# Scaling softmax weights by their reciprocal sums before their transposes, in a hand-scheduled two-layer diffusion block

## The chip, the core and the metric

The kernel runs on one core of a Trainium2 chip. The metric is device time in microseconds (us), from three timed runs before the change; beside them stands one profiled execution of the same program, from which every duration below is read. PE is TensorE (matmuls and transposes), PEld its weight loads, DVE is VectorE, ACT is ScalarE, POOL is GpSimd and SP is SyncE; the last two issue the DMAs here. All engines execute their own instructions strictly in the order in which the program lists them.

## The reference

Two layers of a block with two parallel branches over 512 latent tokens and 256 context tokens, width 1024. The change touches the attention branch alone: 8 query heads in two key groups, head width 128.

```
s = einsum('bqhgd,bkhd->bhgqk', q_blk, keys) * scale
p = softmax(s, axis=-1)
o = einsum('bhgqk,bkhd->bqhgd', p, vals)
```

Latent queries see all 768 keys, context queries only the 256 context keys. Layer 0 needs both kinds of query, layer 1 only the latent ones. The rest (input projection, rotary turns, a long convolution through Fourier tables, gates, output projection, SwiGLU feed-forward) is the same before and after.

## The kernel before

Activations lie with channels on the partitions and tokens along the free axis. Every large product runs as three matmuls (`mm3`): each operand is split in a high part and a low part, and hi·hi, hi·lo and lo·hi are summed in one PSUM tile. A split (`split`) is one ACT copy (the high part) and one DVE subtraction (the low part).

The order of the work is not written by hand. The kernel is a set of Python generators: one main `program`, one per weight load, attention lanes, rotary chunks, splits. A class `Order` keeps a rough clock for each engine. A generator yields what its next step needs (tiles written, free slots of a tile pool, events); among those that can go on, the one with the lowest priority number does. Splits have -5, attention lanes 4, the main program 5, so lanes go ahead of query projections and gates whenever they are ready, and the main program fills what they leave. The result is one fixed order for each engine. Whatever changes an attention step's cost, needs or slots can therefore change the order of everything beside it.

Slots: 37 tiles `s` of 768 columns, 13 tiles `f` and a few others of 1024, 8 PSUM tiles `ps`. Layer 1 needs four `s` slots for each of its four query chunks; each attention unit takes two for its weights `Ps`.

An attention unit (`attn_part`) is one head and 256 queries, as two blocks of 128 (i = 0, 1). There are 24 units in layer 0 (16 latent, 8 context) and 16 in layer 1, all latent: 32 latent and 8 context units in all. A unit's steps:

1. Scores, queries on the partitions: for a latent unit twelve matmuls into three PSUM tiles (`ps<-f,s`, widths 512 and 256, since keys lie in `f` tiles and queries in `s` tiles).
2. Maxima (`mx`), negated and scaled (`nb`) on DVE; exponentials on ACT into `Ps`, their row sums into `sm`.
3. The reciprocal sums `ri` on DVE (`ri<-sm`, `ri<-ri`).
4. For each pair of key tiles four transposes of the weights (`ps<-ident,s`), a split of the result into an `f` tile, and six matmuls with the values (`ps<-f`, width 256), which sum up the output O, head channels on the partitions and queries along the free axis.
5. After the last of them the reciprocal sums, one number for each query, are spread over the partitions by two more transposes (`ps<-ident,ri`), copied by ACT to `rb` (in the slot of `Ps[0]`), multiplied into O by DVE, and the result is split into the query's own tile: ACT `qh`, DVE `ql`. Then the slots are given back, and the lane takes its next unit.

Beside the lanes run the main program's query chunks (`tok_chunk`, `ps<-hi,s` and `ps<-lo,s`, width 256), the rotary chunk of each (`rope_chunk`: on DVE a sum of squares `ss`, ten small instructions on `rs` and `rq`, four passes over 1024 columns), the gates and merges (`ps<-s,hi`, `ps<-s,lo`), and the splits of the arriving weights (`lo<-raw,hi`).

Of the kernel before, what the change touches and what calls it, by code (L numbers as in the profile page):

```python
# [19 lines left out]
P = 128  # L20
# [44 lines left out]
class Order:  # L65
    """Puts the work of several generators into one program order.

    A generator yields what its next step needs: tiles that were written, free
    slots ("tag", n) or Events. Rough costs of the instructions emitted so far
    say when these are there; of the generators that can go on, the one with  # L70
    the lowest priority number does.
    """

# [5 lines left out]

    @staticmethod  # L80
    def span(ap):
        step = ap.ap[0][0]
        lo = ap.offset % step if step else ap.offset
        return ap.tensor.name, lo, lo + 1 + sum((n - 1) * abs(st) for st, n in ap.ap[1:])

# [15 lines left out]
    def run(self, eng, cost, outs, ins, late=0.15, born=None, after=0.0):  # L101
        start = max(self.now[eng], after)
        if born is not None:
            start = max(start, self.born.get(born.tensor.name, 0.0))
        for ap in ins:
            if ap.tensor.name in self.writes:
                start = max(start, self.after(ap, eng))
        for ap in outs:
            start = max(start, self.born.get(ap.tensor.name, 0.0))
        end = start + cost  # L110
        self.now[eng] = end
        for ap in ins:
            n = ap.tensor.name
            self.used[n] = max(self.used.get(n, 0.0), end)
        for ap in outs:
            n, lo, hi = self.span(ap)
            w = [x for x in self.writes.get(n, ()) if not (lo <= x[0] and x[1] <= hi)]
            self.writes[n] = w + [(lo, hi, end, late, eng)]
            self.used[n] = max(self.used.get(n, 0.0), end)
# [7 lines left out]
    def give(self, tag, i, tile_):  # L127
        self.free[tag].append((self.used.get(tile_.tensor.name, 0.0), i))

# [57 lines left out]
RING = 4096  # L187
SLOTS = {"raw": 5, "hi": 4, "lo": 4, "s": 37, "f": 13, "ps": 8}


def hyena_body(ctx, tc, I, out):
# [6 lines left out]

    # ------------------------------------------------------------- tiles and instructions
    def new(tag, dt=F32, n=None):  # L200
        kept = tag == "s"
        od.kept += kept
        tag = {"t": "s"}.get(tag, tag)
        size = {"s": TOK, "ps": 512}.get(tag, 1024)
        p = psp if tag == "ps" else sp
        free, i = od.take(tag)
        t = p.tile([P, n or size], dt, tag=f"{tag}{i}", name=tag)
        od.born[t.tensor.name] = free
        tags[t.tensor.name] = tag, i, kept
        return t  # L210

    def drop(*tiles):
        for t in tiles:
            tag, i, kept = tags[t.tensor.name]
            od.kept -= kept
            od.give(tag, i, t)
# [71 lines left out]
    def rsqrt(y, u):  # L288
        """y becomes (u / RS) ** -0.5."""
        t = cst.tile(list(u.shape), F32, tag="rq", name="rq", bufs=2)  # L290
        ts(y.bitcast(I32), u.bitcast(I32), 1, ALU.logical_shift_right)
        ts(y.bitcast(I32), y.bitcast(I32), -1.0, ALU.mult, float(0x5F3759DF), ALU.add)
        tt(t, y, y, ALU.mult)
        tt(t, t, u, ALU.mult)
        stt(t, t, -10.0 / 3.0, t, ALU.add, ALU.mult)
        stt(y, t, 5.0, y, ALU.add, ALU.mult)
        stt(t, y, -0.5 / RS, y, ALU.mult, ALU.mult)
        tt(t, t, u, ALU.mult)
        stt(y, t, 1.5, y, ALU.add, ALU.mult)
# [5 lines left out]

    # ------------------------------------------------------------- weights, in the order of use
    plan = []
# [61 lines left out]

    # ------------------------------------------------------------- constants  # L370
    silc = cst.tile([P, KD, 2], F32, name="silc")
# [11 lines left out]

    # ------------------------------------------------------------- modulation
    mod = [[cst.tile([P, 48], F32, name=f"mod{l}{s}") for s in range(2)] for l in range(DEPTH)]
# [78 lines left out]

    # ------------------------------------------------------------- norm
    class Sums:
        """The squares of a residual's tiles, summed as they become final."""

# [68 lines left out]

    # ------------------------------------------------------------- projections
    def spans_of(nt):
# [49 lines left out]
    def parts(acts, seg, kept, stay, end, evac):  # L589
        """The output tiles for a part of the tokens; weights that stay serve the next part, first of all."""  # L590
        if kept:
# [8 lines left out]

    # ------------------------------------------------------------- hyena filters
    h3_dram = tc.dram_tile([FH, SEQ], F32, name="h3d")
# [44 lines left out]
    class Tabs:  # L647
        """DFT tables, two of 2 KB a slot: the odd ones stay, the even ones are swapped."""

# [112 lines left out]

    # ------------------------------------------------------------- hyena branch
    hy_dram = [tc.dram_tile([P, 4, TOK], F32, name=f"hyd{l}") for l in range(DEPTH)]
# [149 lines left out]

    # ------------------------------------------------------------- q, k, v
    def tok_chunk(h, nt, evac):
# [102 lines left out]

    # ------------------------------------------------------------- attention  # L1020
    def attn_part(q, kT, v, kvh, q0, k0):
        qh, ql = q
# [25 lines left out]
        for i in range(2):  # L1048
            act(Ps[i][:, c0:c0 + CTX], Sc[:, 256 * i:256 * i + 256], AF.Exp, scale=SCALE, bias=nb[:, i:i + 1],
                accum_out=sm[:, 0, i:i + 1])  # L1050
        drop(Sc, *Sl)
        if lat:
            tt(ri, sm[:, 0, :], sm[:, 1, :], ALU.add)
            recip(ri, ri)
        else:
            recip(ri, sm[:, 0, :])
        hs = slice(HD * kvh, HD * kvh + HD)
        O = None
# [5 lines left out]
        def pv(kp):  # L1064
            pt = pts[kp]
            for kk in range(2):
                kt = k0 // P + 2 * kp + kk
                c = slice(256 * kk, 256 * kk + 256)
                mm3(O[:, 0:256], v[0][kt][:, hs], v[1][kt][:, hs], pt[0][:, c], pt[1][:, c],
                    kp == 0 and kk == 0, kp == nk // 2 - 1 and kk == 1)  # L1070
            drop(pt[0])

        for kp in range(nk // 2):
# [9 lines left out]
            if kp:  # L1083
                if O is None:
                    yield [("ps", 1)]
                    O = new("ps")
                yield list(pts[kp - 1]) + vs(kp - 1)
                pv(kp - 1)
        if O is None:
            yield [("ps", 1)]  # L1090
            O = new("ps")
        yield list(pts[-1]) + [ri] + vs(nk // 2 - 1)
        pv(nk // 2 - 1)
        for i in range(2):
            tr(O[:, 256 + P * i:256 + P * i + P], ri[:, i:i + 1].to_broadcast([P, P]))
        rb = Ps[0]
        act(rb[:, 0:256], O[:, 256:512])
        yield [rb[:, 0:256]]
        tt(rb[:, 0:256], O[:, 0:256], rb[:, 0:256], ALU.mult)
        drop(O)  # L1100
        yield [rb[:, 0:256]]
        act(qh[:, q0:q0 + 256], rb[:, 0:256])
        yield [qh[:, q0:q0 + 256]]
        tt(ql[:, q0:q0 + 256], rb[:, 0:256], qh[:, q0:q0 + 256], ALU.subtract)
        drop(*Ps)

    def attn_lane(units, qT, kT, v, left, done, after):
        while units:
            hd, part = units.pop(0)
            yield [ev for ev in after[hd]]  # L1110
            yield from attn_part(qT[hd], kT[hd // 4], v, hd // 4, 256 * part, 0 if part < 2 else SEQ)
            left[hd] -= 1
            done[hd].set = left[hd] == 0

    # ------------------------------------------------------------- layers
    gate_dram = [tc.dram_tile([16, P, TOK], F32, name=f"gated{l}") for l in range(DEPTH)]
# [100 lines left out]
    def program():  # L1217
# [29 lines left out]
        for l in range(DEPTH):  # L1247
# [3 lines left out]
            stag = ((0, 256), (256, 512)) if last else ((0, SEQ), (SEQ, TOK))  # L1251
            # norm, hyena columns
            if l == 0:
# [4 lines left out]
            if l == 0:  # L1258
                # the residual's loads go before those of the tables
                yield [xs[-1][:, SEQ:TOK]]  # L1260
# [23 lines left out]
            for j in islice(gates, EARLY[l]):  # L1284
                yield from gate_job(l, h, nt, j)
            # q, k, v
            stop.set = True
# [18 lines left out]
            yield from tok_chunk(h, TOK, v_evac)  # L1306
            # attention beside the queries and gates
            qT = []
# [24 lines left out]
            yield [here]  # L1333
            # merge, output projection
            if l == 0:
# [24 lines left out]
            drop(*[x for p in mg for x in p])  # L1360
            # feed-forward
            for gi, (f0, fn) in enumerate(GROUPS):
# [86 lines left out]

# ---------------------------------------------------------------- host layout  # L1450
def _split(x64):
# [125 lines left out]
```

## Time and profile before

| | |
|---|---|
| Timed runs | 2189.72, 2190.36, 2190.59 us; median 2190.36 us |
| Profiled execution, span from first to last instruction | 2187.6 us |
| PE busy | 2146.5 us, 98% |
| DVE busy | 1365.3 us, 62% |
| ACT busy | 744.3 us, 34% |
| Layer 0, 285 to 625 us: PE, DVE, ACT busy | 337.06, 222.42, 151.81 us |
| Layer 1, 1500 to 1730 us: PE, DVE, ACT busy | 225.75, 149.91, 117.98 us |

The profile gives the profiled execution by its span alone; the median of the timed runs lies 2.8 us above that span. The two windows hold nearly all of the attention. A busy time merges overlapping instructions, and consecutive instructions of one engine do overlap in the trace, so the cost of one in a run of equals is the distance between starts and not its duration.

### The profile page before, as it was taken

The page shows a single profiled execution, that of the slowest core. Times are in us where ns is not written, and L with a number is a line of the kernel's source. Part 1 is how long each engine was busy: PE and PEld are TensorE (multiplying, and loading weights), DVE is VectorE, ACT ScalarE, POOL GpSimd, SP SyncE. Part 2 cuts the span into 40 slices and gives each one's busy share as a digit, 9 for nine tenths or more (in the row PEclk, how much of TensorE's full clock was granted, in tenths as well). Part 3 has the DMA queues.
Part 4 walks back from the last instruction along what each step waited for, and adds up shares of the span by engine and source line. Part 5 has one row for each costly group of instructions (what it writes and reads, how often), then busy time and mean ns, then how long its engine had stood idle before and what let it go on. Part 6 is the DMA issues. An engine that isn't in the chain of part 4 may idle for free.

```text
span 2187.6 us, 31896 instructions
## 1 busy us (share of the span) xinstructions
PE 2146.5 (98%) x12849; PEld 1888.5 (86%) x12849; DVE 1365.3 (62%) x2510; ACT 744.3 (34%) x1350; POOL 116.8 (5%) x218
## 2 busy tenths in 40 slices
PE   7999999999999999999999999999999999999997
PEld 2889999999888888888888887899888898888887
DVE  5879766665796799733333477766756666434345
ACT  3432234444522421121221334224455443222222
POOL 2111100000100000000000011200001000000000
PEclk9999999999999999999999999999999999999999
DMA  9334521112465257812112232522213433323221
GB/s 327 100 117 151 192 81 46 37 51 80 152 229 183 78 196 239 306 44 74 65 50 82 102 111 91 182 85 73 102 49 121 158 111 99 106 83 111 80 95 57
DMA packets 83060, 256.84 MB, mean 117 GB/s; under 512 B 10668, under 2 KB 15183, under 8 KB 82912
## 3 DMA queue, kind: packets, MB, share of 16 engines
q1 hardware_dynamic: 63840, 197.43, 26.7%
q0 software_dynamic: 19072, 57.36, 8.0%
q8 instruction: 101, 1.65, 0.3%
q14 instruction: 47, 0.39, 0.1%
HBM read 232.07 MB, written 22.68 MB: 116 GB/s over the span
## 4 chain that ended last, share of the span: by engine, by line
PE 92%; DVE 4%; issue 2%; ACT 1%; DMA 1%; POOL 0%; SPq 0%; DVEq 0%; ACTq 0%; POOLq 0%
PE ps L230 89%; PE ps L240 3%; DVE s L250 1%; DVE f L254 1%; ACT s L244 1%; DVE s L254 1%; DMA s<-gated 0%; DVE mx L265 0%; DVE lo L254 0%; DMA s<-in_fw 0%; DMA f<-in_wmodf 0%; ACT hi L244 0%; ACT f L244 0%; POOL s L273 0%; DVE ss L265 0%
## 5 line engine op out<-in xcount | busy, mean ns | idle before, releaser
L230 PE MATMUL ps<-s,hi 128*128 128x512 f32 (+1 forms) x4288 | 1136.2, 353 | 7.5 <-ACT s L244 3.6
L230 PEld LDWEIGHTS ps<-s,hi 128*128 128x128 f32 x4288 | 748.5, 190 | 113.9 <-ACT s L244 4.9
L230 PE MATMUL ps<-s,lo 128*128 128x512 f32 (+1 forms) x2144 | 751.6, 351 | 1.0 <-DVE lo L254 1.0
L230 PEld LDWEIGHTS ps<-s,lo 128*128 128x128 f32 x2144 | 406.5, 190 | 55.5 <-DVE lo L254 1.4
L244 ACT ACTIVATE hi<-raw 128x1024 fp32r<-128x1024 f32 (+2 forms) x272 | 267.3, 994 | 354.1 <-PE ps L230 217.7
L254 DVE TENSOR_TENSOR lo<-raw,hi 128x1024 fp32r<-128x1024 f32 (+2 forms) x272 | 308.0, 1142 | 48.8 <-ACT hi L244 46.8
L230 PE MATMUL ps<-f,hi 128*128 128x512 f32 (+1 forms) x1184 | 297.0, 341 | 0.0
L250 DVE SCALAR_TENSOR_TENSOR s<-s,ps 128x512 f32<-128x512 f32 (+1 forms) x184 | 107.0, 587 | 280.1 <-ACT s L244 150.4
L244 ACT ACTIVATE s<-ps 128x512 f32<-128x512 f32 (+5 forms) x228 | 107.9, 492 | 353.5 <-PE ps L230 273.8
L230 PEld LDWEIGHTS ps<-f,hi 128*128 128x128 f32 x1184 | 205.0, 190 | 25.4
L230 PE MATMUL ps<-f,lo 128*128 128x512 f32 (+1 forms) x592 | 201.4, 340 | 0.0
L230 PE MATMUL ps<-hi,s 128*128 128x256 f32 x1024 | 191.6, 285 | 0.4 <-ACT s L244 0.4
L250 DVE SCALAR_TENSOR_TENSOR s<-ps,mod,s 128x256 f32<-128x256 f32 (+1 forms) x144 | 83.1, 586 | 154.2 <-PE ps L230 154.0
L230 PEld LDWEIGHTS ps<-hi,s 128*128 128x128 f32 x1024 | 162.0, 192 | 0.6 <-ACT s L244 0.6
L230 PE MATMUL ps<-f 128*128 128x256 f32 (+1 forms) x1014 | 145.5, 290 | 7.5 <-DMA f<-in_fw 3.9
L244 ACT ACTIVATE f<-ps 128x512 fp32r<-128x512 f32 (+2 forms) x164 | 90.2, 585 | 170.0 <-PE ps L230 127.2
L230 PE MATMUL ps<-lo,s 128*128 128x256 f32 x512 | 144.9, 283 | 0.0
L230 PEld LDWEIGHTS ps<-f 128*128 128x128 f32 (+1 forms) x1014 | 131.0, 190 | 12.4 <-DVE f L254 4.4
L244 ACT ACTIVATE s<-ps,nb 128x256 f32<-128x256 f32 (+1 forms) x144 | 80.7, 567 | 146.4 <-DVE nb L259 142.5
L244 ACT ACTIVATE s<-s 128x256 f32<-128x256 f32 (+4 forms) x161 | 76.6, 484 | 157.7 <-DVE s L250 125.3
L230 PEld LDWEIGHTS ps<-f,lo 128*128 128x128 f32 x592 | 112.2, 189 | 12.6
L254 DVE TENSOR_TENSOR f<-ps,f 128x512 fp32r<-128x512 f32 (+2 forms) x144 | 90.2, 654 | 41.2 <-ACT f L244 40.2
(119 smaller groups left out, 1858.9 us busy)
## 6 DMA issues: line engine op xcount, KB each, us to landing
raw<-in_w_gu SPq DMA_DIRECT2D x88, 512.0 KB, 3.3
raw<-in_wmodt SPq DMA_DIRECT2D x80, 512.0 KB, 4.3
raw<-in_w_down SPq DMA_DIRECT2D x48, 384.0 KB, 3.1
raw<-in_w_gate SPq DMA_DIRECT2D x32, 512.0 KB, 3.4
raw<-in_w_hy SPq DMA_DIRECT2D x24, 512.0 KB, 4.4
raw<-in_w_qkv SPq DMA_DIRECT2D x24, 512.0 KB, 3.3
raw<-in_w_out SPq DMA_DIRECT2D x24, 512.0 KB, 3.2
f<-in_tab POOLq DMA_DIRECT2D x40, 256.0 KB, 5.6
```

Source lines behind the costliest of these rows:

```text
L230: nc.tensor.matmul(out=o, lhsT=l, rhs=r, start=start, stop=stop)
L240: nc.tensor.transpose(o, x, ident[0:n, 0:n])
L244: nc.scalar.activation(out=o, in_=i, func=f, **kw)
L250: nc.vector.scalar_tensor_tensor(out=o, in0=a, scalar=s, in1=b, op0=op0, op1=op1)
L254: nc.vector.tensor_tensor(out=o, in0=a, in1=b, op=op)
```

## The change

The reciprocal sums are applied to the weights, where a query is a partition and the sum is a per-partition number, ahead of the transposes. Step 3 gains two DVE multiplications per unit, in place on `Ps` (768 columns for a latent unit, 256 for a context unit). Step 5 loses its two transposes, the ACT copy `rb` and the DVE multiplication. The output's split reads O in PSUM directly and becomes a generator of its own (`out`, priority 0), so that the lane goes on to its next unit without waiting for it. The slots of `Ps` are given back before the last six value matmuls instead of after the split. A new `yield` stands between the exponentials and the reciprocal sums, so that `Order` lists the latter only when the exponentials are due.

```diff
         drop(Sc, *Sl)
+        yield [x[:, 0:P * nk] for x in Ps]
         if lat:
             tt(ri, sm[:, 0, :], sm[:, 1, :], ALU.add)
             recip(ri, ri)
         else:
             recip(ri, sm[:, 0, :])
+        for i in range(2):
+            ts(Ps[i][:, 0:P * nk], Ps[i][:, 0:P * nk], ri[:, i:i + 1], ALU.mult)
...
-        yield list(pts[-1]) + [ri] + vs(nk // 2 - 1)
+        drop(*Ps)
+        yield list(pts[-1]) + vs(nk // 2 - 1)
         pv(nk // 2 - 1)
-        for i in range(2):
-            tr(O[:, 256 + P * i:256 + P * i + P], ri[:, i:i + 1].to_broadcast([P, P]))
-        rb = Ps[0]
-        act(rb[:, 0:256], O[:, 256:512])
-        yield [rb[:, 0:256]]
-        tt(rb[:, 0:256], O[:, 0:256], rb[:, 0:256], ALU.mult)
-        drop(O)
-        yield [rb[:, 0:256]]
-        act(qh[:, q0:q0 + 256], rb[:, 0:256])
-        yield [qh[:, q0:q0 + 256]]
-        tt(ql[:, q0:q0 + 256], rb[:, 0:256], qh[:, q0:q0 + 256], ALU.subtract)
-        drop(*Ps)
+
+        def out():
+            act(qh[:, q0:q0 + 256], O)
+            yield [qh[:, q0:q0 + 256]]
+            tt(ql[:, q0:q0 + 256], O, qh[:, q0:q0 + 256], ALU.subtract)
+            drop(O)
+            left[hd] -= 1
+            done[hd].set = left[hd] == 0
+
+        od.spawn(out(), 0)
```

The other lines of the change are the bookkeeping of names and sizes in `Order` and `new` (the same sizes as before) and comments that were taken out; line numbers move by four.

The instructions' order differs in the two attention stages and nowhere else. In layer 1, where the query chunks meet the lanes, TensorE's order before reads as follows (`ps<-f,s` scores, `ps<-ident,s` transposes of weights, `ps<-hi,s` and `ps<-lo,s` query projections):

```order
L230 MATMUL ps<-f,s 128x512 x3
L230 MATMUL ps<-f,s 128x256 x3
L240 MATMUL ps<-ident,s 128x128 x8
L230 MATMUL ps<-hi,s 128x256
L230 MATMUL ps<-lo,s 128x256
L230 MATMUL ps<-hi,s 128x256 x2
```

This is the end of the second unit's scores; 42 query matmuls stand between these transposes and the next ones, and 12 more before the first value matmuls. After the change the lanes run ahead there; this is the end of the fourth unit's scores and what comes next (`ps<-f` value matmuls, `ps<-ident,f` transposes of a rotary chunk):

```order
L234 MATMUL ps<-f,s 128x512 x3
L234 MATMUL ps<-f,s 128x256 x3
L244 MATMUL ps<-ident,s 128x128 x16
L234 MATMUL ps<-f 128x256 x12
L244 MATMUL ps<-ident,s 128x128 x4
L234 MATMUL ps<-f 128x256 x6
L244 MATMUL ps<-ident,s 128x128 x4
```

Four units' scores now stand with only 9 and 24 query matmuls between them, and no projection follows until two more units' scores are done: the work that used to lie between a unit's transposes and its value matmuls has gone from there.

On VectorE, before, at the same place (`f<-ps,f` the low halves of the transposed weights, `ss<-f` the start of a rotary chunk):

```order
L254 TENSOR_TENSOR ri<-sm 128x2
L269 RECIPROCAL ri<-ri 128x2
L254 TENSOR_TENSOR f<-ps,f 128x512 x2
L254 TENSOR_TENSOR lo<-raw,hi 128x1024 x2
L254 TENSOR_TENSOR f<-ps,f 128x512 x2
L265 TENSOR_REDUCE ss<-f 128x8
```

After the change (`s<-s,ri` are the new multiplications; first the stretch up to the rotary chunk, then the end of its small instructions):

```order
L263 TENSOR_SCALAR s<-s,ri 128x768 x2
L258 TENSOR_TENSOR lo<-raw,hi 128x1024 x2
L258 TENSOR_TENSOR ri<-sm 128x2
L273 RECIPROCAL ri<-ri 128x2
L263 TENSOR_SCALAR s<-s,ri 128x768 x2
L258 TENSOR_TENSOR f<-ps,f 128x512 x2
L269 TENSOR_REDUCE ss<-f 128x8
```

```order
L258 TENSOR_TENSOR rq<-rq,ss 128x8
L254 SCALAR_TENSOR_TENSOR rs<-rq,rs 128x8
L258 TENSOR_TENSOR f<-f,rs 128x1024
L258 TENSOR_TENSOR f<-f 128x1024
L258 TENSOR_TENSOR f<-ps,f 128x512 x2
```

The first unit's low halves stand ahead of the rotary chunk, the second unit's behind its small instructions and two of its passes; before, the four low halves shown all stood ahead of it.

More of the change, by code (lines that the diff above doesn't have):

```diff
@@ L78, in __init__, with span, name @@
         self.kept = 0
-    @staticmethod
-    def span(ap):
+    def span(self, ap):
         step = ap.ap[0][0]
         lo = ap.offset % step if step else ap.offset
-        return ap.tensor.name, lo, lo + 1 + sum((n - 1) * abs(st) for st, n in ap.ap[1:])
+        hi = lo + 1 + sum((n - 1) * abs(st) for st, n in ap.ap[1:])
+        return ap.tensor.name, lo, hi
+    def name(self, ap):
+        return self.span(ap)[0]
     def ready(self, ap):
@@ L103, in run @@
         if born is not None:
-            start = max(start, self.born.get(born.tensor.name, 0.0))
+            start = max(start, self.born.get(self.name(born), 0.0))
         for ap in ins:
-            if ap.tensor.name in self.writes:
+            if self.name(ap) in self.writes:
                 start = max(start, self.after(ap, eng))
         for ap in outs:
-            start = max(start, self.born.get(ap.tensor.name, 0.0))
+            start = max(start, self.born.get(self.name(ap), 0.0))
         end = start + cost
@@ L112, in run @@
         for ap in ins:
-            n = ap.tensor.name
+            n = self.name(ap)
             self.used[n] = max(self.used.get(n, 0.0), end)
@@ L127, in give @@
     def give(self, tag, i, tile_):
-        self.free[tag].append((self.used.get(tile_.tensor.name, 0.0), i))
+        self.free[tag].append((self.used.get(self.name(tile_), 0.0), i))
     def when(self, needs):
@@ L188 @@
 SLOTS = {"raw": 5, "hi": 4, "lo": 4, "s": 37, "f": 13, "ps": 8}
+WIDE = {"raw": 1024, "hi": 1024, "lo": 1024, "s": TOK, "f": 1024}
 def hyena_body(ctx, tc, I, out):
@@ L203, in new @@
         tag = {"t": "s"}.get(tag, tag)
-        size = {"s": TOK, "ps": 512}.get(tag, 1024)
-        p = psp if tag == "ps" else sp
         free, i = od.take(tag)
-        t = p.tile([P, n or size], dt, tag=f"{tag}{i}", name=tag)
-        od.born[t.tensor.name] = free
-        tags[t.tensor.name] = tag, i, kept
+        pl, size = (psp, 512) if tag == "ps" else (sp, WIDE[tag])
+        t = pl.tile([P, n or size], dt, tag=f"{tag}{i}", name=tag)
+        nm = t.tensor.name
+        od.born[nm] = free
+        tags[nm] = tag, i, kept
         return t
@@ L213, in drop @@
         for t in tiles:
-            tag, i, kept = tags[t.tensor.name]
+            tag, i, kept = tags[od.name(t)]
             od.kept -= kept
@@ L1018, in last_use, with attn_part @@
         drop(*tiles)
-    def attn_part(q, kT, v, kvh, q0, k0):
+    def attn_part(q, kT, v, kvh, q0, k0, hd, left, done):
         qh, ql = q
@@ L1068, in pv @@
                 c = slice(256 * kk, 256 * kk + 256)
-                mm3(O[:, 0:256], v[0][kt][:, hs], v[1][kt][:, hs], pt[0][:, c], pt[1][:, c],
+                mm3(O, v[0][kt][:, hs], v[1][kt][:, hs], pt[0][:, c], pt[1][:, c],
                     kp == 0 and kk == 0, kp == nk // 2 - 1 and kk == 1)
@@ L1085, in attn_part @@
                     yield [("ps", 1)]
-                    O = new("ps")
+                    O = new("ps")[:, 0:256]
                 yield list(pts[kp - 1]) + vs(kp - 1)
@@ L1090, in attn_part @@
             yield [("ps", 1)]
-            O = new("ps")
-        yield list(pts[-1]) + [ri] + vs(nk // 2 - 1)
+            O = new("ps")[:, 0:256]
+        drop(*Ps)
+        yield list(pts[-1]) + vs(nk // 2 - 1)
         pv(nk // 2 - 1)
-        for i in range(2):
-            tr(O[:, 256 + P * i:256 + P * i + P], ri[:, i:i + 1].to_broadcast([P, P]))
-        rb = Ps[0]
-        act(rb[:, 0:256], O[:, 256:512])
-        yield [rb[:, 0:256]]
-        tt(rb[:, 0:256], O[:, 0:256], rb[:, 0:256], ALU.mult)
-        drop(O)
-        yield [rb[:, 0:256]]
-        act(qh[:, q0:q0 + 256], rb[:, 0:256])
-        yield [qh[:, q0:q0 + 256]]
-        tt(ql[:, q0:q0 + 256], rb[:, 0:256], qh[:, q0:q0 + 256], ALU.subtract)
-        drop(*Ps)
+        def out():
[6 more added lines that the diff above has]
+        od.spawn(out(), 0)
     def attn_lane(units, qT, kT, v, left, done, after):
@@ L1110, in attn_lane @@
             yield [ev for ev in after[hd]]
-            yield from attn_part(qT[hd], kT[hd // 4], v, hd // 4, 256 * part, 0 if part < 2 else SEQ)
-            left[hd] -= 1
-            done[hd].set = left[hd] == 0
+            yield from attn_part(qT[hd], kT[hd // 4], v, hd // 4, 256 * part, 0 if part < 2 else SEQ, hd, left, done)
     gate_dram = [tc.dram_tile([16, P, TOK], F32, name=f"gated{l}") for l in range(DEPTH)]
```

## The prediction

> **What bounds the kernel now.** I read the page first, then the busy times and TensorE's wait lists of the two attention windows, then the groups by shape, and last the timelines around a unit's end.
>
> ```profile
> span 2187.6 us, 31896 instructions
> PE 2146.5 (98%) x12849; PEld 1888.5 (86%) x12849; DVE 1365.3 (62%) x2510; ACT 744.3 (34%) x1350; POOL 116.8 (5%) x218
> PE 92%; DVE 4%; issue 2%; ACT 1%; DMA 1%; POOL 0%; SPq 0%; DVEq 0%; ACTq 0%; POOLq 0%
> ...
> 285.00:625.00 340.00, 337.06 (x2368) 313.51 (x2366) 222.42 (x504) 151.81 (x363) 17.33 (x31) 1.00 0.26 86
> 1500.00:1730.00 230.00, 225.75 (x1387) 199.49 (x1386) 149.91 (x322) 117.98 (x270) 17.78 (x33) 1.00 0.27 91
> ```
>
> TensorE is busy for 98% of the span and makes up 92% of the chain that ended last. Work taken off it shortens the program at once; work added to another engine costs only where TensorE comes to wait for it. So two things count: the transposes removed, and the waits removed or made. The last two rows are the attention windows (PE, PEld, DVE, ACT, POOL busy): DVE is busy for 65% of each, ACT for half.
>
> The wait lists, TensorE in 285 to 625 us (layer 0) and in 1500 to 1730 us (layer 1):
>
> ```profile
> PE ps L230 <- DVE f L254: 1.8, 2, 1.1
> PE ps L230 <- ACT s L244: 1.0, 2, 0.6
> PE ps L240 <- DVE s L254: 0.2, 1, 0.2
> ...
> PE ps L230 <- ACT s L244: 1.4, 1, 1.4
> PE ps L240 <- ACT s L244: 1.3, 2, 0.7
> PE ps L230 <- DVE f L254: 0.8, 1, 0.8
> PE ps L230 <- DVE s L254: 0.7, 1, 0.7
> ```
>
> 3.0 us in layer 0 and 4.2 us in layer 1, 7.2 us in all: that is all that a better order of the attention can win back. The reader should note how little this is beside 570 us of windows; the old order hides every unit's chain.
>
> **The transposes removed.** 32 + 8 units, two each:
>
> ```profile
> L240 PE MATMUL ps<-ident,ri 128*128 128x128 f32 x80 | 15.2, 271 | 0.0
> 1702.82 0.63 PE L230 MATMUL ps<-s,hi 128*128 128x512 f32 x2
> 1703.29 0.39 PE L230 MATMUL ps<-s,lo 128*128 128x512 f32 x1
> 1703.51 0.87 PE L230 MATMUL ps<-f 128*128 128x256 f32 x6
> 1704.22 0.38 PE L240 MATMUL ps<-ident,ri 128*128 128x128 f32 x2
> 1704.36 4.45 PE L230 MATMUL ps<-f,s 128*128 128x512 f32 x24
> 1708.64 0.63 PE L230 MATMUL ps<-s,hi 128*128 128x512 f32 x2
> ```
>
> A mean of 271 ns is a duration, not a cost, because matmuls overlap. By starts, three 512-wide matmuls take 0.69 us (1702.82 to 1703.51), 0.23 each, and six 256-wide ones 0.71 us, 0.12 each. From the pair's start to 1708.64 lie 4.42 us, and the 24 score matmuls in it (twelve of each width) account for 12 × 0.23 + 12 × 0.12 = 4.2 us. The pair costs 0.22 to 0.24 us; 40 pairs at 0.23 make **-9.2 us**. The ends are 80 × 0.11 = 8.8 us (the step from one transpose to the next) and the group's 15.2 us busy.
>
> The Trainium skill, "TensorE: Matmul & The Clock Gate", section on the PE-mode transpose, puts a transpose in a kernel at about 275 ns. The duration in this trace agrees; used as a price it would make the term -22 us, and the starts above speak against that use.
>
> **Other edits off the path.** Removed: 40 DVE multiplications and 40 ACT copies. The split now reads PSUM where it read SBUF.
>
> ```profile
> L254 DVE TENSOR_TENSOR s<-s,ps 128x256 f32<-128x256 f32 x40 | 14.0, 414 | 5.6 <-PE ps L230 4.1 <-ACT f L244 1.5
> L244 ACT ACTIVATE s<-ps 128x256 f32<-128x256 f32 x91 | 35.1, 385 | 109.1 <-PE ps L230 62.9 <-PE ps L240 46.1
> 1725.70 0.38 PE L240 MATMUL ps<-ident,ri 128*128 128x128 f32 x2
> 1727.53 0.96 PE L230 MATMUL ps<-s,hi 128*128 128x512 f32 x2 [1.44 <-ACT s L244]
> ```
>
> TensorE waits for them once, at the end of layer 1's attention: from the last pair at 1725.70 to the merge at 1727.53. That 1.4 us is in the list above. The new order puts 372 gate and merge matmuls behind the last value matmul, where 150 stood: 222 × 0.23, some 51 us of cover, so this wait goes. Elsewhere the removals only lighten ACT (15 us) and DVE (16.6 us), which TensorE's own work hides.
>
> **The multiplications added.** The trace has no in-place multiplication of 768 columns by a per-partition number. The nearest rows:
>
> ```profile
> L261 DVE TENSOR_SCALAR f<-f 128x512 f32<-128x512 f32 x6 | 2.6, 426 | 0.2
> L261 DVE TENSOR_SCALAR f<-f 64x256 f32<-64x256 f32 x6 | 1.7, 285 | 0.2
> L254 DVE TENSOR_TENSOR s<-s 128x768 f32<-128x768 f32 x12 | 11.4, 954 | 0.2
> ```
>
> The same operation from SBUF grows by 141 ns for 256 columns, so 768 should take 0.57 us; the two-tensor operation of that size takes 0.95. I take 0.60, near the row of the same operation, and keep 0.95 as the upper end. 64 × 0.60 plus 16 short ones at 0.3 are 43 us, and 26 us more than the removed multiplications: nothing on average, with DVE at 65%, but not where vector work is bunched.
>
> **Waits made: the new order in layer 1.** The lane no longer waits for its own output, and `Ps` is free earlier, so lanes run ahead of the query chunks. From the end of the second unit's scores to the second six value matmuls (which need the low half that now stands behind the rotary chunk) I count the instructions of both engines in the new order. The distances between starts come from these rows:
>
> ```profile
> 335.01 1.28 DVE L265 TENSOR_REDUCE mx<-ps 128x2 f32<-128x512 f32 x2
> 400.99 2.34 DVE L254 TENSOR_TENSOR lo<-raw,hi 128x1024 fp32r<-128x1024 f32 x2
> 403.25 0.68 DVE L254 TENSOR_TENSOR f<-ps,f 128x512 fp32r<-128x512 f32 x1
> 403.85 0.68 DVE L265 TENSOR_REDUCE ss<-s 128x4 f32<-128x512 f32 x1
> 404.56 0.17 DVE L261 TENSOR_SCALAR ss<-ss 128x4 f32<-128x4 f32 x1
> 404.76 0.17 DVE L259 TENSOR_SCALAR rs<-ss 128x4 int32<-128x4 int32 x1
> 404.97 0.17 DVE L261 TENSOR_SCALAR rs<-rs 128x4 int32<-128x4 int32 x1
> ```
>
> Long ones of 512 columns follow each other at 0.60 us (403.25 to 403.85), those of 1024 at 1.13 (two from 400.99 to 403.25), small dependent ones at 0.20.
>
> - VectorE: 9 maxima (three units) 5.4; 30 small ones (12 for maxima, 8 for four pairs of sums and reciprocals, 10 rotary) 6.0; 8 new multiplications 4.8; 5 of 1024 columns (two weight splits, the rotary sum, two of its passes) 5.65; 3 low halves 1.8. Sum 23.7 us, in one queue.
> - TensorE: the scores of two units 4.2; 9 query matmuls 1.1; 16 transposes at 0.11, 1.75; the first six value matmuls 0.7. Sum 7.7 us.
>
> Nothing else stands in TensorE's queue there, so it waits 23.7 - 7.7 = **16.0 us**, in steps ahead of the first units' transposes and value matmuls. This is a lower bound for that stretch: VectorE's waits for exponentials would add to it. Behind the waiting matmuls are queued all further scores and the query chunk that would feed them; so it isn't made up. Without the eight multiplications the same order would wait 11.2 us.
>
> **Waits made: layer 0.** One stretch is alike. From one unit's scores to the next unit's transposes VectorE has three maxima 1.8, four smalls 0.8, two weight splits 2.25, a 512-column rotary chunk for context queries with its sum, ten smalls and two passes 3.8, three output parts 1.55, and the sums with two multiplications 1.6: 11.8 us. TensorE has 42 matmuls of 256 columns 5.05 and 12 transposes 1.3: 6.4 us. The wait is 5.4 us. Two later stretches, counted likewise, give 0.4 (4.3 against 3.9) and 1.7 (11.1 against 9.4). In all **+7.5 us**.
>
> **Waits of the common kind.** The 7.2 us of old waits go with their order, and some of their kind come back in the rest of the new one, by ACT and DVE chains that no sum of one engine shows: between 0 and 7.2; I take 2.3, since attention is then shorter by some 50 us in layer 1 and TensorE is late already.
>
> **The clock.** After idle time TensorE runs slower for a while:
>
> ```profile
> 1304.68 0.61 PE L230 MATMUL ps<-ones,s 128*128 128x2 f32 x4 [3.23 <-DVE s L254]
> 1306.06 0.63 PE L230 MATMUL ps<-s,lo 128*128 128x512 f32 x1
> 1308.92 0.40 PE L230 MATMUL ps<-s,lo 128*128 128x512 f32 x1
> 1305.00:1312.00 7.00, 7.00 (x26) 5.15 (x25) 5.78 (x23) 3.19 (x7) 0.58 (x2) 0.76 0.60 168
> ```
>
> After a wait of 3.23 us the granted clock was 0.76 over the next 7 us, and a 512-wide matmul took 0.63 us instead of 0.40: 7 × (1 - 0.76) = 1.7 us lost. The 16 us of waiting should do the same once, partly under VectorE's lead: +1.5 us, between 0 and 3.4 (twice).
>
> The Trainium skill, "TensorE: Matmul & The Clock Gate", section on what is actually happening, has the clock halved after an idle window of about 3.4 us and full again after a busy one, which by itself would make this term 1.7 us. The window above agrees.
>
> **Sum.** -9.2 - 7.2 + 16.0 + 7.5 + 2.3 + 1.5 = +10.9 us. The profiled span of 2187.6 becomes 2198.5; the runs' median lies 2.8 above the span, so 2201.3, **2201 us**.
>
> **The rivals.**
>
> - *Faster: VectorE gets through the stretch in layer 1 as fast as TensorE.* Small instructions of several units stand side by side there and may follow each other faster than those of one dependent chain, from which I took 0.20 us. Against it: thirty of them make 6.0 of the 23.7 us, and the rest has starts measured on independent work; the same counting on the old order gives 0.6, 0.7 and 1.1 us at three places of layer 1, where its list has 4.2 in all, so it counts too little and not too much. With no wait there and no clock loss the sum is -6.6 us, 2184 us. It decides below a wait of 6.6 us; under 2.2 the result is measurably faster. Chance 0.08.
> - *No change:* the stretch waits 2 to 11 us, because VectorE's lead is half hidden, and the transposes pay for it: about 2190 us. Chance 0.12.
> - *Each transpose frees its full duration:* 80 × 271 ns = 21.7 instead of 9.2, and the rest as forecast: 2201.3 - 12.5 = 2189 us. The price on the Trainium skill's page named above would lead here. The starts contradict it. Chance 0.02.
> - *Slower still:* the multiplications run at the two-tensor rate. Eight of them in the stretch add 8 × 0.35 = 2.8 us, those in layer 0 another 1.5; with the clock lost twice and the common waits at 7.2 the sum is +22, 2212 us. Chance 0.10.
>
> **Numbers.** The forecast itself has 0.68, with its own range 2195 to 2207. 0.2% (4.4 us) is about what a measurement of this kernel can tell from no change. Slower by more: 0.68 + 0.10 = 0.78; within: 0.14; faster by more: 0.08. The range takes in most of "no change" and the slower end: 2187 to 2213.
>
> **What would show it.** The pairs on `ri` are gone and TensorE has 80 instructions fewer. The multiplications show as a group of 64 at about 0.6 us: at 0.95 that choice was wrong. TensorE's wait list in layer 1 gains some 16 us on DVE at about 1.52 ms, in a few waits before transposes and value matmuls, with a granted clock under 1 there; layer 0 gains about 5 us near 0.41 ms. The idle time of DVE before `ri` (57.6 us in 32 waits before) falls. If the layer-1 list stays under 7 us, the counting was wrong and the time is at or below 2190.
>
> ```profile
> L254 DVE TENSOR_TENSOR ri<-sm 128x2 f32<-128x2 f32 x32 | 5.1, 161 | 57.6 <-ACT s L244 57.6
> ```

## The result: slower, and the profile after

| | before | after |
|---|---|---|
| Timed runs, us | 2189.72, 2190.36, 2190.59 | 2206.71, 2207.10, 2207.75, 2210.59 |
| Median, us | 2190.36 | 2207.43 |
| Ratio, 95% interval | | 1.0083, 1.0070 to 1.0096 |

The kernel became 17 us slower; the forecast said 11. A fourth timed run of before took 2648.76 us, against 2189.72 to 2190.59 for the other three, and counts in no comparison here. The profiled execution of after is its slowest run (2210.59 us), with a span 21.2 us longer than that of before. The page's head, and then, asked for by stretch of time (length, then PE, PEld, DVE, ACT and POOL busy, the granted clock, DMA share, GB/s), the two attention windows and the 36 us of layer 1 where the loss sits:

```profile
span 2208.8 us, 31739 instructions
PE 2148.8 (97%) x12769; PEld 1889.9 (86%) x12769; DVE 1391.6 (63%) x2550; ACT 732.7 (33%) x1310; POOL 117.2 (5%) x218
```

```profile
285.00:625.00 340.00, 332.74 (x2318) 309.24 (x2317) 246.63 (x548) 146.25 (x341) 17.83 (x31) 0.99 0.28 94
1500.00:1735.00 235.00, 215.84 (x1310) 192.14 (x1310) 159.75 (x334) 109.74 (x250) 16.07 (x30) 0.95 0.23 76
1525.00:1561.00 36.00, 22.55 (x127) 20.09 (x125) 30.22 (x70) 16.27 (x40) 0.00 (x0) 0.72 0.10 30
```

80 matmuls fewer, 26 us more on VectorE, 12 less on ScalarE: the inventory is as counted. In the third stretch TensorE works for 22.55 of 36 us, and at a mean clock of 0.72. TensorE's wait lists, first layer 0 (285 to 625 us), then layer 1 (1500 to 1735 us); us in total, times, the longest:

```profile
PE ps L244 <- DVE ri L258: 2.2, 1, 2.2
PE ps L244 <- DVE s L263: 1.5, 2, 1.3
PE ps L234 <- DVE s L258: 1.5, 1, 1.5
PE ps L244 <- ACT s L248: 1.1, 2, 0.8
PE ps L234 <- ACT s L248: 0.8, 1, 0.8
```

```profile
PE ps L234 <- DVE f L258: 9.0, 2, 5.2
PE ps L244 <- DVE s L263: 4.7, 3, 2.6
PE ps L244 <- ACT s L248: 3.9, 2, 3.2
PE ps L234 <- ACT s L248: 0.6, 1, 0.6
```

7.1 us instead of 3.0 in layer 0, 18.8 instead of 4.2 in layer 1 (the four rows shown and three of 0.2). The first two rows of layer 1 hold 13.7 us in five waits. Four of them, 12.6 us, stand within 21 us of the timeline of TensorE (start, length, instruction, in brackets the idle time ahead of it and what ended it):

```profile
1527.98 2.26 PE L234 MATMUL ps<-f,s 128*128 128x512 f32 x12
1531.28 1.42 PE L244 MATMUL ps<-ident,s 128*128 128x128 f32 x8 [1.04 <-DVE s L263]
1535.29 2.19 PE L244 MATMUL ps<-ident,s 128*128 128x128 f32 x8 [2.58 <-DVE s L263]
...
1541.50 1.65 PE L234 MATMUL ps<-f 128*128 128x256 f32 x6 [3.81 <-DVE f L258]
1548.36 1.44 PE L234 MATMUL ps<-f 128*128 128x256 f32 x5 [5.21 <-DVE f L258]
```

VectorE in the same stretch is one unbroken queue from 1525.00 to 1548.8 us:

```profile
1525.00 1.29 DVE L269 TENSOR_REDUCE mx<-ps 128x2 f32<-128x512 f32 x2 [1.14 <-PE ps L234]
...
1530.51 1.15 DVE L263 TENSOR_SCALAR s<-s,ri 128x768 f32<-128x768 f32 x2
...
1540.76 1.28 DVE L258 TENSOR_TENSOR f<-ps,f 128x512 fp32r<-128x512 f32 x2
1541.96 1.21 DVE L269 TENSOR_REDUCE ss<-f 128x8 f32<-128x1024 f32 x1
...
1545.22 1.22 DVE L258 TENSOR_TENSOR f<-f,rs 128x1024 f32<-128x1024 f32 x1
1546.48 1.22 DVE L258 TENSOR_TENSOR f<-f 128x1024 f32<-128x1024 f32 x1
1547.62 1.28 DVE L258 TENSOR_TENSOR f<-ps,f 128x512 fp32r<-128x512 f32 x2
```

The first low halves (1540.76) release the value matmuls at 1541.50; the second (1547.62) stand behind the start of the rotary chunk and release those at 1548.36. This is the wait that the prediction counted: 23.4 us from the queue's start to those value matmuls, against 23.7 counted. By form, the multiplications and the sums:

```profile
L263 DVE TENSOR_SCALAR s<-s,ri 128x768 f32<-128x768 f32 x64 | 36.8, 617 | 1.4 <-DVE ri L273 0.3
L258 DVE TENSOR_TENSOR ri<-sm 128x2 f32<-128x2 f32 x32 | 5.0, 156 | 12.7 <-ACT s L248 12.6
```

617 ns each; two take 1.15 us (1530.51), so the step is 0.53 to 0.57. VectorE's idle time ahead of the sums fell from 57.6 to 12.7 us, and the program became slower: filling that idle time was no gain in itself.

**Where the 21 us lie.** Let the lag of a point be its measured start minus the steps of all matmuls ahead of it in program order (0.23 us at 512 columns, 0.12 at 256, 0.11 a transpose): it grows where TensorE waits or runs slow, and its growth is comparable between orders. After minus before, the lag grew by 5.6 us more in layer 0's attention (11.3 against 5.7), by 21.9 more in layer 1's (27.3 against 5.4), by 2.1 more between them and 1.1 ahead of them, where the change touches nothing. With 8.7 us of transposes gone these make +22.0; the spans differ by 21.2.

### The profile page after: what moved, and what is told of

Its sections match the earlier page's. It is cut to its first block, busy times and chain, and to the rows that moved or that the text cites. A ratio compares the mean times of both kernels' runs of the same rounds, so it can differ in the third digit from the quotient of the medians.

```text
span 2208.8 us, 31739 instructions
## 1 busy us (share of the span) xinstructions
PE 2148.8 (97%) x12769; PEld 1889.9 (86%) x12769; DVE 1391.6 (63%) x2550; ACT 732.7 (33%) x1310; POOL 117.2 (5%) x218
## 4 chain that ended last, share of the span: by engine, by line
PE 73%; issue 20%; DVE 2%; POOL 1%; DMA 1%; ACT 0%; POOLq 0%; DVEq 0%; ACTq 0%
PE ps L234 71%; PE ps L244 2%; DVE s L254 1%; DVE s L258 0%; DMA f<-in_tab 0%; POOL gated L277 0%; POOL s L277 0%; POOL f L277 0%; ACT s L248 0%; POOL spec L277 0%; DMA s<-hyd 0%; DVE mx L269 0%; DVE lo L258 0%; DMA f<-in_dec 0%; POOL hyd L277 0%
## 5 line engine op out<-in xcount | busy, mean ns | idle before, releaser
L234 PEld LDWEIGHTS ps<-f,lo 128*128 128x128 f32 x592 | 112.2, 189 | 12.6
L269 DVE TENSOR_REDUCE mx<-ps 128x1 f32<-128x512 f32 (+1 forms) x104 | 68.5, 684 | 77.2 <-PE ps L234 77.2
L258 DVE TENSOR_TENSOR f<-ps,f 128x512 fp32r<-128x512 f32 (+2 forms) x144 | 90.4, 654 | 39.9 <-ACT f L248 39.5
```

The lines of the kernel that those rows point to most:

```text
L234: nc.tensor.matmul(out=o, lhsT=l, rhs=r, start=start, stop=stop)
L258: nc.vector.tensor_tensor(out=o, in0=a, in1=b, op=op)
L269: nc.vector.tensor_reduce(out=o, in_=a, op=op, axis=AX.X)
```

## The experiments

Theory L is the prediction's: the output's own task and the early release of `Ps` let lanes run ahead. Theory Y puts the order down to the new yield between exponentials and sums, which lets other generators' vector work in there. Theory M: the multiplications' own time on VectorE. Lag growth is given for layer 0's and layer 1's attention, from each run's profile.

| kernel | median us | ratio to before, 95% | lag, layer 0 | lag, layer 1 |
|---|---|---|---|---|
| before | 2190.36 | | 5.7 | 5.4 |
| after | 2207.43 | 1.0083 (1.0070 to 1.0096) | 11.3 | 27.3 |
| yield alone | 2230.36 | 1.0186 (1.0169 to 1.0203) | 8.8 | 40.5 |
| no yield | 2205.06 | 1.0069 (1.0054 to 1.0084) | 21.9 | 14.7 |
| narrow | 2202.90 | 1.0061 (1.0046 to 1.0076) | 10.4 | 22.4 |
| two lanes | 2193.72 | 1.0017 (1.0008 to 1.0026) | 10.2 | 15.3 |
| output in the lane | 2228.12 | 1.0170 (1.0155 to 1.0186) | 13.6 | 42.9 |
| task alone | 2199.12 | 1.0041 (1.0027 to 1.0054) | 7.7 | 12.4 |
| three entries | 2178.63 | 0.9942 (0.9930 to 0.9955) | 3.7 | 5.2 |
| three entries on before | 2212.02 | 1.0095 (1.0082 to 1.0109) | 6.4 | 26.3 |
| three entries, transposes back | 2185.88 | 0.9983 (0.9974 to 0.9992) | 3.7 | 5.1 |
| three entries, narrow | 2175.13 | 0.9931 (0.9917 to 0.9944) | 3.6 | 4.5 |
| three entries, twice | 2202.55 | 1.0060 (1.0044 to 1.0075) | 16.7 | 16.0 |
| no yield, narrow | 2196.60 | 1.0028 (1.0017 to 1.0040) | 18.2 | 10.8 |

**1. The yield alone**, on the kernel before:

```diff
         drop(Sc, *Sl)
+        yield [x[:, 0:P * nk] for x in Ps]
```

> The kernel before with one line added: the lane yields after its exponentials until the weights are written, as the changed kernel does ahead of its reciprocals. No multiplication added, no transpose removed, output in the lane as before. Theory Y (the yield lets other tasks put their vector work, the rotary chunk above all, between a unit's exponentials and its reciprocals, and this order is the loss): slower, 2205 to 2222 us, with over 15 us on TensorE's wait list of layer 1's attention, most of it on VectorE within 30 us around 1.53 ms. Theory L, that of the prediction (lanes run ahead because the output is a task of its own and the weights' tiles are freed early): neither is in this kernel, so 2187 to 2194. Theory M (the multiplications' vector time): also 2187 to 2194.

2230.4 us: one line, not one instruction added or removed, and 40 us lost, more than twice the whole change's loss. Layer 1's list (1490 to 1745 us):

```profile
PE ps L230 <- DVE f L254: 13.3, 8, 5.5
PE ps L240 <- ACT s L244: 6.3, 6, 1.7
PE ps L240 <- DVE f L254: 5.4, 1, 5.4
PE ps L230 <- ACT s L244: 2.9, 2, 1.6
```

L and M both said no change; Y holds in sign. In place it holds in part: two waits of 5.5 and 5.4 us for VectorE end at 1544.7 and 1554.4 us, but more than half of the list's 28.9 us stands later, up to 1.74 ms, and the time is above Y's upper end. What the yield does can also be read from VectorE's idle time ahead of the latent units' sums: 57.6 us before, 22.9 with the yield alone. Other work now stands where VectorE used to wait for the exponentials.

**2. The change without the yield.**

> The changed kernel without that yield; multiplications, own output task and early release stay. Theory Y: the waits near 1.53 ms fall from about 13 us to under 4; the vector work is still added, so smaller waits stand elsewhere (about 10 us in layer 0, about 8 near 1.7 ms): 2195 to 2204 us. Theory L: the stretch near 1.53 ms stays, 2205 to 2210. Theory M: same vector time, 2205 to 2210.

The stretch at 1.53 ms is gone, as Y said: the longest wait within 30 us of it is 1.5 us. VectorE's idle time ahead of the sums is back at 56.6 us. But the time is 2205.1, 1.1 beyond Y's upper end. Layer 1's lag halves (27.3 to 14.7), and layer 0's doubles (11.3 to 21.9). Layer 0, 285 to 640 us:

```profile
PE ps L244 <- DVE f L258: 3.8, 1, 3.8
PE ps L244 <- ACT s L248: 3.6, 2, 3.3
PE ps L234 <- DVE s L258: 3.4, 1, 3.4
```

So the yield makes the stretch in layer 1; without it there is another loss, most of it in layer 0, and 14.7 of the 17 us remain. The yield is the cause of that stretch and not of the whole difference in time.

**3. The change with narrow multiplications, its order unchanged.**

```diff
-            ts(Ps[i][:, 0:P * nk], Ps[i][:, 0:P * nk], ri[:, i:i + 1], ALU.mult)
+            x = Ps[i][:, 0:P * nk:P // 2]
+            nc.vector.tensor_scalar(out=x, in0=x, scalar1=ri[:, i:i + 1], scalar2=None, op0=ALU.mult)
+            od.run("DVE", 0.065 + P * nk * 0.0006, [Ps[i][:, 0:P * nk]], [Ps[i][:, 0:P * nk]])
```

The last line still tells `Order` the full cost, so that the order stays.

> The changed kernel in its own order, with each multiplication on every 64th column only (12 columns of 768; the other weights stay unscaled). VectorE has some 30 us less to do. Theory M: the loss goes, at or below 2190 us. Theories Y and L: the order costs, not the 30 us: the stretch near 1.53 ms still waits 9 to 13 us, 2199 to 2205 us.

2202.9 us: VectorE is busy for 1366.2 us, 25 less, and 4.5 of the 17 us come back (the intervals of the two ratios overlap, their runs, 2206.7 to 2210.6 and 2202.1 to 2204.7, do not). M as the main cause falls.

**4. Two lanes in layer 1.** `LANES = (2, 5)` becomes `(2, 2)`; every instruction is the same.

> The changed kernel with two lanes at the start of layer 1's attention instead of five; all else as it is, the same instructions in another order. Theories Y and L: fewer units can put their maxima and sums ahead of each other's low halves: one wait of about 6 us is left near 1.53 ms, the half clock behind it is shorter, the 3 us wait near 1.62 ms goes: 2191 to 2197 us. Theory M: the same vector work, 2205 to 2210.

2193.7 us: an order with the same work is 13.7 us faster, within L's and Y's range. One long wait is left in layer 1:

```profile
PE ps L244 <- DVE f L258: 6.4, 1, 6.4
PE ps L244 <- DVE s L263: 1.7, 1, 1.7
```

**5 and 6. Task and release taken back together, and the task alone.** In the first the changed kernel has the output's steps back in the lane, and `drop(*Ps)` behind them (the diff); in the second the kernel before has its own output steps (copy, multiplication, split) wrapped in a task `out` of priority 0, with `drop(*Ps)` at its end.

```diff
-        drop(*Ps)
         yield list(pts[-1]) + vs(nk // 2 - 1)
         pv(nk // 2 - 1)
-        def out():
...
-        od.spawn(out(), 0)
+        act(qh[:, q0:q0 + 256], O)
+        yield [qh[:, q0:q0 + 256]]
+        tt(ql[:, q0:q0 + 256], O, qh[:, q0:q0 + 256], ALU.subtract)
+        drop(O)
+        drop(*Ps)
+        left[hd] -= 1
+        done[hd].set = left[hd] == 0
```

> The changed kernel with its output back in the lane and the weights' tiles freed only after it, as before; the yield and the multiplications stay. Theory L (the own output task and the early release let lanes run ahead, and that is the loss): the stretch near 1.53 ms goes, 2185 to 2195 us. Theory Y (the yield made that order; the task and the release rather help): the stretch stays and more waits follow it in layer 1, where the output's two dependent steps hold the lane again: 2215 to 2235 us.

> The kernel before with its output steps (the turned sums' copy, the multiplication, the split) in a task of its own; nothing else of the change. Theory L: the lanes run ahead as in the changed kernel, a wait of over 8 us stands near 1.53 ms: 2200 to 2212. Theory Y: no such wait; a few of 1 to 3 us more in both attentions: 2190 to 2198.

2228.1 us with both taken back: they are not the loss, they save 21 us by the medians (19 by the ratios) once the yield is there. The task alone costs 9 us (1.1 above Y's range), with waits of up to 2.7 us near the end of layer 1's attention, and no wait stands near 1.53 ms. L falls as the cause of that stretch: experiment 1 has neither edit and the loss, experiment 2 has both and no stretch. The early release was not tried by itself.

**7 and 8. Another order for the same instructions**, and the same entries on the kernel before:

```diff
-LANES, MORE_LANES = (2, 5), (0, 3)
+LANES, MORE_LANES = (2, 2), (0, 3)
...
-MIX = ((2, 0, 1, 0), (0, 1, 0, 0))
+MIX = ((2, 0, 1, 0), (0, 0, 1, 0))
...
-                ..., 0 if t0 == 2 else 4, count), ROPE)
+                ..., 0 if t0 == 2 else 4, count), ROPE if l else -6)
```

> The changed kernel, the same instructions in another order by three entries: two lanes at the start of layer 1's attention instead of five, layer 0's rotary chunks at priority -6 instead of 2, and in layer 1 one gate job after the third query chunk instead of the second. If the order is the loss: no wait of over 2 us is left in either attention, the transposes' 9 us are gained and 3 to 6 us of waits remain above those of before: 2180 to 2187 us, faster than before. If the vector time of the multiplications is the loss: 2200 to 2210.

> The kernel before with the same three entries. If they are good for any kernel, it is faster than before too, 2180 to 2188. If they only fit the changed lane: one wait of about 9 us near 1.53 ms and several of 1 to 3 us around 1.7 ms: 2200 to 2212.

2178.6 us, below the expected 2180 to 2187: faster than before by 11.7, and faster than the changed kernel by 28.8 with not one instruction of the engines more or less. All waits of layer 1's attention:

```profile
PE ps L234 <- DVE s L258: 1.6, 1, 1.6
PE ps L244 <- ACT s L248: 1.0, 1, 1.0
PE ps L234 <- ACT s L248: 0.7, 1, 0.7
```

The lags are those of before or less (3.7 and 5.2 us), so the transposes' gain is kept. On the kernel before the same entries cost 21.7 us, with a wait of 9.0 us in layer 1: an order fits one lane and not another. VectorE's idle time ahead of the latent units' sums is 7.0 us in the fast order, less than the changed kernel's 12.7, and 57.3 us with the same entries on the kernel before: it doesn't tell which kernel is fast. Of the three entries only the lanes were tried singly, in experiment 4; what the other two give apart stays open.

**9. The transposes put back** in the fast order, their result unread (`full` is the whole PSUM tile of which O is the first half):

```diff
         pv(nk // 2 - 1)
+        for i in range(2):
+            nc.tensor.transpose(full[:, 256 + P * i:256 + P * i + P], ri[:, i:i + 1].to_broadcast([P, P]), ident)
```

> The kernel of the three entries (2178.6 us), with the two transposes of each unit's reciprocals put back behind its last value matmul, in the same place of the same order; nobody reads their result. This prices the term of -9.2 us by itself. By the step between starts (0.11 us each, 0.23 a pair): 8.8 to 9.2 us slower than that kernel, 2186 to 2190 us. If a transpose costs its duration of 271 ns: 21.7 us slower, 2198 to 2202. If TensorE hides it behind the weight loads: no change, 2177 to 2181.

```profile
L1105 PE MATMUL ps<-ident,ri 128*128 128x128 f32 x80 | 15.2, 271 | 0.0
```

2185.9 us, 7.2 more than without them by the medians, 9.0 by the ratios (0.9983 - 0.9942), 4 to 14 by the ends of their intervals; the spans differ by 7.3. The time is just below the first case's 2186. The 80 last 271 ns each and cost about 0.1 us each. The price by duration, 21.7, is out; so is a price of nothing.

**10, 11 and 12. The vector work**: narrow in the fast order; in the fast order with a second multiplication by 1.0 behind each (`L1065` below); narrow without the yield.

> The kernel of the three entries, with each multiplication on every 64th column only (12 of 768; the other weights stay unscaled), the order unchanged. If VectorE's time costs nothing where the order covers it: 2176 to 2180 us. If the multiplications cost in every order what they cost in the changed kernel (4.5 us between 2207.4 and 2202.9): 2172 to 2175.

> The kernel of the three entries, with a second multiplication of the same size (by 1.0) behind each, the order unchanged: 80 instructions and some 41 us more on VectorE, standing between a unit's sums and its transposes. If the cover ahead of the transposes is used up by then, TensorE waits at many units by 0.7 to 1 us and in two or three places by more: 2192 to 2203 us. If there is cover to spare: 2178 to 2184.

> The changed kernel without its yield (2205.1 us as measured), with each multiplication on every 64th column only (12 of 768; the other weights stay unscaled). If the multiplications' vector time is what costs in that order: 2188 to 2193. If the order costs there too, and the vector time 4 to 7 us as in the changed kernel: 2197 to 2202, with waits of about 10 us left in layer 0.

Taking 25 us of vector work away gains 3.5 us in the fast order (2175.1 lies between the two expected ranges, and the intervals overlap, so 0 isn't excluded), 4.5 in the changed kernel's, 8.5 in that without the yield (2196.6, just below the second case's 2197). Adding 39.5 us (1429.2 busy against 1389.7) to the fast order costs 23.9, within the first case's range. There TensorE waits for the second multiplication 17 times in layer 0 and 10 times in layer 1:

```profile
PE ps L244 <- DVE s L1065: 7.8, 17, 1.2
...
PE ps L244 <- DVE s L1065: 4.5, 10, 0.7
```

So the fast order covers one pair of multiplications between a unit's sums and its transposes: its two wait lists hold 5.6 us in all, none of it for a multiplication. A second pair comes out at more than half its length. In the order without the yield, 6.2 us of loss against before remain when 25 of the multiplications' 42 us are gone: there, too, order and work both count.

## Why the prediction was right, and where it was not

The sign, the mechanism (TensorE waiting for a longer VectorE queue in the new order) and the place were right, and 2207.4 lies in the range of 2187 to 2213, but 0.4 above the forecast's own 2195 to 2207. Which edit made that order was wrong.

- **Transposes, -9.2.** Right: 8.7 us by the steps of the 80 that are gone, 7.2 to 9.0 by experiment 9. The price by duration (271 ns, the rival taken from the Trainium skill, "TensorE: Matmul & The Clock Gate", section on the PE-mode transpose) is excluded: the page's figure agrees with the duration in the trace and isn't what a transpose costs in a row of matmuls.
- **The stretch in layer 1, +16.0, and the clock, +1.5.** Right as a pair: from 1531 us to 1561 us the lag grows from 81.0 to 99.3, 18.3 us against 17.5. The queue took 23.4 us, against 23.7. The rival that VectorE goes through it faster falls with this. Of the rival "slower still" the multiplications at 0.95 fall; its slow clock (3.4 us) and its common waits (7.2) came close to what the next lines show. The split of the 18.3 was off: 12.6 us are waits and the rest is half clock, which lasted 20.5 us:

```profile
1534.00:1554.50 20.50, 10.19 (x44) 9.33 (x45) 18.01 (x38) 6.64 (x16) 0.00 (x0) 0.50 0.17 52
1548.30:1554.50 6.20, 6.14 (x29) 6.14 (x30) 4.36 (x7) 1.19 (x2) 0.00 (x0) 0.50 0.00 0
```

  Up to 1548.3 the slow matmuls lie mostly under VectorE's lead and shorten the waits; the second row is 6.2 us of unbroken matmul work at 0.50 from the last wait on, 3.1 us lost instead of 1.5.
- **Layer 0, +7.5.** Right in size: the lag grows by 11.3 us, where before had 5.7, of which 3.0 were the old waits; 5.7 - 3.0 + 7.5 = 10.2. The waits come to 7.1 us against 7.5 counted, four of them, 4.8 us, near 0.41 ms where 5.4 were counted; the largest is 2.2 us before transposes. The half clock behind them, which the forecast counted for layer 1 alone, makes up most of the rest (0.89 over 410 to 425 us, 1.7 us lost).
- **Common waits, +2.3: the term that was too small.** After the stretch TensorE's lag in layer 1 grows from 99.3 to 107.0. Three short waits, 2.0 us in all, stand at 1561 to 1564, and one that no sum had found at 1618.84 (from the wait back through ACT to VectorE):

```profile
1618.84 0.66 PE L244 MATMUL ps<-ident,s 128*128 128x128 f32 x4 [3.17 <-ACT s L248]
1618.01 0.69 ACT L248 ACTIVATE s<-ps,nb 128x512 f32<-128x512 f32 x1 [10.81 <-DVE nb L263]
1609.79 3.69 DVE L258 TENSOR_TENSOR f<-f 128x1024 f32<-128x1024 f32 x4
1616.31 1.28 DVE L269 TENSOR_REDUCE mx<-ps 128x2 f32<-128x512 f32 x2
```

  A rotary chunk's passes, then another unit's multiplications and a weight split, stand ahead of a unit's maxima; ACT idles 10.81 us for them. The transposes' own weights had been multiplied by 1615.3, so what TensorE waits for is taken to be the PSUM tile that ACT's exponentials then free. The sum over DVE's queue alone could not see it, because it goes on through ACT and a slot. With the slow clock behind it the lag grows by 7.7 us there, where 2.3 were allowed for both layers. By the spans the forecast was 10.3 us short (2198.5 against 2208.8): 5.4 from this, 1.1 in layer 0, 0.8 in the stretch, and 3.2 ahead of and between the attentions, where the change touches nothing (10.5 in all, by rounded lags). By the medians it was 6.1: after's median lies 3.2 below its profiled run, and the profiled run of before lay about 1.0 below its median. That is chance and no merit of the forecast; a run's time lies about 1.8 us above its span in every run on record that gives both, and the 2.8 that the forecast added held that 1.0 as well.
- **The cause, as the prediction put it, was wrong.** It said that the lanes run ahead because they don't wait for their output and `Ps` is free earlier. Experiments 1, 2, 5 and 6 show the yield as the cause of the stretch instead: alone it costs 40 us, and with it in place the two that were blamed save some 20. It is not the cause of all of the loss, as experiment 2 shows; that the order is for the most part, and not the work, experiment 7 shows. I had read the new order, counted it well, and given it to the two largest edits beside it instead of asking of each edit what order it makes alone.
- **The multiplications, 0.60 us each and nothing on average.** The size held (0.617). "Nothing on average" didn't quite: 25 us of vector work are worth 3.5 (0 not excluded) to 8.5 us by order, and in the changed kernel the 4.5 of experiment 3 stand against the 4.8 (16.0 - 11.2) that the prediction gave to the stretch alone; the narrow form still takes 238 ns of VectorE, so it can't show the whole.

## What to carry to other kernels

Where a planner sets the order, try each yield, task and release by itself, in the order that it makes: here a yield without an instruction cost 40 us, and three entries of a table turned a loss of 17 us into a gain of 11.7. Before calling an edit bad, retune the order around it, and put the tuned entries on the old kernel too, or the gain may be the tuning's alone (here they cost the old kernel 21.7 us). Filling an engine's idle time ahead of an instruction (57.6 us to 12.7 here) isn't a gain unless the engine that bounds the program waits less; it was 7.0 us in the fastest of the full kernels and 57.3 in a slow one.

## What the runs showed of the hardware beyond expectation

- The same wait can bring half clock for one step or for two. Ahead of layer 1, in code that no edit touches, TensorE waits 3.23 us for VectorE in the kernel before and in the changed kernel. Around its end the granted clock (the third number from the right) falls to 0.50, for 3.4 us in the first and for 6.8 us in the second:

```profile
1305.35:1308.74 3.39, 3.39 (x10) 2.58 (x10) 2.46 (x14) 1.03 (x3) 0.26 (x1) 0.50 1.03 283
1305.33:1312.14 6.81, 6.20 (x18) 4.98 (x18) 5.19 (x21) 2.81 (x6) 1.50 (x3) 0.50 0.80 214
```

  A second wait follows some 10 us later: 3.04 us in the kernel before, 3.28 in the fast order. With both waits, the granted clock over 30 us is 0.89 in the kernel before (first row) and 0.77 in the fast order (second row); 0.12 of 30 us are 3.6 us:

```profile
1300.00:1330.00 30.00, 23.73 (x99) 18.20 (x98) 27.47 (x66) 16.91 (x31) 4.31 (x8) 0.89 0.22 62
1295.00:1325.00 30.00, 25.14 (x85) 18.99 (x86) 25.26 (x60) 15.63 (x28) 2.48 (x5) 0.77 0.21 57
```

  In all fourteen traces every stretch of half clock but the last, which the end of the trace cuts short, is a whole number of times 3.41 us long (1 to 6 times), and within a trace all begin on one grid of that step. Where a wait falls on the grid is the likely reason for the difference; no run moves a wait along it. So kernels differ by a few us where no edit touches them: the lag between the attentions was 21.2 to 24.7 us over the fourteen profiles, least where half clock there lasted 6.8 us and most where it lasted 17.1. The Trainium skill, "TensorE: Matmul & The Clock Gate", section on what is actually happening, has windows of about 3.4 us that run freely, which fits.
- In the changed kernel half clock lasted 20.5 us in one piece where four waits of 1 to 5 us followed each other with little matmul work between them; it ended 6.2 us after the last wait.
- Cover runs out suddenly: in the fast order taking away 25 of the multiplications' 42 us gained 3.5 us, and 39.5 us more cost 23.9, though VectorE was then busy for only 65% of the span.
